# A state-space layer's constants: the elementwise work put on VectorE alone, and the lag products laid side by side on TensorE's columns

## The chip, the cores and the metric

The kernel runs on one core of one Trainium2 chip. The metric is the device time of one execution in microseconds. The kernel before takes 2569.31 us, the median of three runs (2568.99 to 2569.63). Five engines work beside each other, each through its own list of instructions in order: TensorE (PE; its weight loads are PEld), VectorE (DVE), ScalarE (ACT), GpSimd (POOL) and SyncE (SP), which issues most of the transfers. They wait for each other by semaphores.

## The reference, cut to what matters

A trunk of four residual layers on 512 positions of 1024 channels. Each layer has a token mixer (Fourier, state space, attention, Fourier) and a SwiGLU feed-forward. The change concerns the state-space mixer (S5) of the second layer, and of it only what depends on the parameters alone: the discretised diagonal system of 64 groups of 16 channels with 64 complex states, in two directions.

```python
def _s5_direction(u, lam_re, lam_im, log_dt, b_re, b_im, c_re, c_im, reverse):
    lam = lax.complex(lam_re, lam_im)
    dt = jnp.exp(log_dt)[:, None]
    lam_bar = jnp.exp(lam * dt)
    b_bar = ((lam_bar - 1.0) / lam)[..., None] * lax.complex(b_re, b_im)
    bu = lax.complex(einsum('bsgp,gnp->bsgn', u, b_bar.real), einsum('bsgp,gnp->bsgn', u, b_bar.imag))
    _, hs = lax.associative_scan(combine, (broadcast(lam_bar), bu), axis=1, reverse=reverse)
    return einsum('gpn,bsgn->bsgp', c, hs).real

y = y_fwd + y_bwd + d_skip * h        # then GELU and a gated linear unit
```

The kernel takes the 512 positions in 64 chunks of 8. Inside a chunk an output depends on an input at a distance (lag) of 0 to 7 positions, before it or behind it, through a 16 x 16 matrix per group and lag: C lam_bar^lag B, for each direction. These matrices, the input weights, the output weights and the angles of the states are what the preparation computes and stores in DRAM.

## The kernel before, in words

All activations lie with channels on the 128 partitions and the 512 positions along the free axis. The layers run one after the other. A feed-forward (`ffn`) has two halves; each half has 11 pairs of products for gate and up (`gemm`, 24 matmuls of 128x128 against 512 columns: 8 steps of three, since each weight is split into a high and a low float32r part), and then 8 blocks of the down product (33 matmuls each). The `Stream` loads a weight chunk of 512 KB into one of three buffers; ScalarE casts it to the high part (`whi`, line 191), VectorE subtracts to get the low part (`wlo`, line 192). When product n is issued, chunk n + 2 is split, and its buffers are those that product n - 1 read.

The preparation of the state-space layer (`s5_prepare`) is a list of closures. Six run in the Fourier layer before; the others are background work of the first feed-forward: `run_bg` is called after each product of the first half and the second, and pops closures at the rate of their number over 54 calls. With 57 closures, three calls pop two. The first 14 compute factors and powers of lam_bar; then come steps over 16 batches b of four groups, as a pipeline: step i issues stages of batches i, i - 1, i - 2 and so on, in two closures.

- `loads(b)`: three transfers on SyncE's queue (`xpw`, `xbj` of 512 KB, `bc` of 128 KB).
- `pool_part(b)`: six products and differences on GpSimd (angles `mph`, halves of the input weights `wtmp`, halves of the readers `ct`), with one rounding on VectorE between them.
- `dve_part(b)`: the input weights `wout`, four operations of 128x512 on VectorE.
- `dve_part2(b)`: the factor times B (`bt`), then `s5bd` by directions, four operations of 64x64; then the readers `ce`, four operations of 128x576.
- `lags(b)`: 8 products of 32 x 144 on TensorE, which the hardware runs as 16 instructions (lines 963 to 966), two copies by ScalarE into `lt` with both directions on 32 partitions, and the stores of `wout`, `mph`, `ce`.
- `lag0(b)`, `last(b)`: one direction's lag 0 is moved by a transfer to the other's partitions, VectorE adds it and the skip term (three operations of 16x64), and the rows go to DRAM (`s5ZS`), from where they are read skewed.

VectorE's order in a pair of the feed-forward is: `wlo`, the product of gate and up (line 500), one closure, `wlo`, two products from PSUM with the norm's factor (lines 474, 477), one closure. All the elementwise helper operations have line 733, so they are told apart by their tiles.

Of the kernel before, what the change touches and what calls it, by code (L numbers as in the profile page):

```python
# [16 lines left out]
P = 128  # L17
# [17 lines left out]
# ---------------------------------------------------------------- host layout  # L35
# [10 lines left out]
def _constants():  # L46
# [3 lines left out]
    c["ones"] = np.ones((P, P), f)  # L50
    bo = np.zeros((P, P), f)
# [13 lines left out]
    # positions 2u and 2u + 1 against the frequencies to 128, and the position 256  # L65
# [39 lines left out]
def _host_arrays(v):  # L105
# [44 lines left out]
    a["d5"] = cc(v["s5_d"][0].reshape(G5, 16).T)  # L150
# [65 lines left out]
class Net:  # L216
# [45 lines left out]
    # ---- weights in order of use  # L262
# [51 lines left out]
    def run_bg(self, slots):  # L314
        """Background work, spread over the slots that are left."""
# [8 lines left out]
    def keep_warm(self, count):  # L324
        """Matmuls without a use, so that TensorE's clock isn't halved by the wait that follows."""
# [10 lines left out]
    def gemm(self, hi, lo, chunk=None, ps=None, ks=range(KT)):  # L336
        """The next chunk's 128 columns against all of hi + lo."""
# [7 lines left out]
    # ---- residual stream and norms  # L345
# [4 lines left out]
    def mirrored(self, m):  # L350
        """Places of H for the positions: those above 256 backwards, 512 - s at 256 + s."""
# [3 lines left out]
    def start(self, nxt):  # L355
        """The first layer's input, as it comes in."""
# [19 lines left out]
    def after_x(self, m, nxt, late=None, defer=False):  # L376
# [38 lines left out]
        else:  # L415
# [5 lines left out]
            if late:  # L421
                # high part on ScalarE; VectorE takes the next sum before it waits for that
# [10 lines left out]
    def next_h(self):  # L433
        """A second place for the next layer's input."""
# [17 lines left out]
    # ---- feed forward  # L452
# [44 lines left out]
    def split_mul(self, hi, lo, t1, t2):  # L497
        """hi + lo = t1 * t2."""
# [5 lines left out]
    # ---- Fourier mixing  # L504
    def fnet(self, l, nxt):
        nc, H, j = self.nc, self.H, l // 3
        with ExitStack() as st:
# [12 lines left out]
            # the positions s = 2u and 2u + 1, then 512 - s for the odd and for the even ones. Position  # L520
            # 256, in the place of 512, is not to be folded: its row is taken apart.
# [6 lines left out]
            # block by block as the input comes in, for the first three tiles of tokens; the last  # L528
            # tile's products then run beside the norm's factors
# [24 lines left out]
            # the factors of the mirrored positions, in their order; zero at the place of 512  # L554
# [10 lines left out]
            def middle(hf, last):  # L565
                """Position 256."""
# [17 lines left out]
            def spread(u, ps, c):  # L584
                """The frequencies above 128 from those below."""
# [30 lines left out]
            def product(m, c):  # L616
                """The mixed channels' product with 128 columns of the weights."""
# [80 lines left out]
    # ---- S5: constants from the parameters, kept in DRAM until layer 1  # L698
# [21 lines left out]
    def s5_prepare(self):  # L720
        """Closures that each issue a part of the preparation."""
# [13 lines left out]
        def begin():  # L735
# [5 lines left out]
            for n in ("er", "ei", "er-"):  # L741
                T(n, [P, 9, 64], keep=True)
            for i in range(2):
                G.memset(T(f"bd{i}", [P, 2, 4, 2, 16], keep=True), 0.0)
            sm["iota"] = self.const("iota", pools["keep"])
            sm["lam"] = self.const("lam", pools["tmp"])
            sm["d5"] = self.const("d5", pools["keep"])
# [26 lines left out]
        def pexp1(x, scale=1.0):  # L774
            """exp(scale * x), to float32's accuracy, begun: x = k ln 2 + r."""
# [44 lines left out]
        def factors1():  # L820
            """(exp(lambda dt) - 1) / lambda."""
# [20 lines left out]
        def factors3():  # L842
            """One chunk's turn back, for the shift of the states."""
# [7 lines left out]
        def powers(ks):  # L851
            def go():
# [61 lines left out]
        def pool_part(b):  # L914
            d = tmp[b]
            pr, pi, xr, xi = d["we"]
            t = d["wt"] = tl("wtmp", [P, 2, 4, P])
            ph = d["ph"] = tl("mph", [P, 4, 64], 3)
            phi = sm["phi0"][:, 4 * b:4 * b + 4]
            tt(G, ph, phi.unsqueeze(2).to_broadcast([P, 4, 64]), sm["iota"].unsqueeze(1).to_broadcast([P, 4, 64]), M)  # L920
            x = t[:, 0, :, 0:64]
# [8 lines left out]
        def dve_part(b):  # L930
            d = tmp[b]
            pr, pi, xr, xi = d["we"]
            w = d["w"] = tl("wout", [P, 4, 2, P], 2)
            tt(V, w[:, :, 0], pr, xr, M)
            tt(V, w[:, :, 0], w[:, :, 0], d["wt"][:, 0], Sb)
            tt(V, w[:, :, 1], pr, xi, M)
            tt(V, w[:, :, 1], w[:, :, 1], d["wt"][:, 1], A)

        def dve_part2(b):
            d = tmp[b]  # L940
            bc = d["bc"]
# [9 lines left out]
            tt(V, ce[:, :, 0], e(b, "er"), c(d, 0), M)  # L951
            tt(V, ce[:, :, 0], ce[:, :, 0], d["ct"][:, 0], Sb)
            tt(V, ce[:, :, 1], e(b, "er-"), c(d, 1), M)
            tt(V, ce[:, :, 1], ce[:, :, 1], d["ct"][:, 1], Sb)

        def lags(b):
            k, h = divmod(b, 2)
            d = tmp[b]
            ce, bd = d["ce"], sm[f"bd{b % 2}"]
            lt = d["lt"] = tl("lt", [32, 4, 9, 16], 2)  # L960
            for g0 in (0, 2):
                ps = self.pst.tile([32, 2, 144], F32, name="pt", tag="pt")
                for g in range(g0, g0 + 2):
                    for ri in range(2):
                        nc.tensor.matmul(ps[:, g - g0, :], bd[:, ri, g].rearrange("p d q -> p (d q)"),
# [787 lines left out]
```

## Time and profile before

| what | value |
|---|---|
| median of three runs | 2569.31 us |
| span of the profiled execution | 2565.2 us (4.1 us less than that median) |
| mean granted TensorE clock | 0.976 |
| busy share PE, DVE, ACT, POOL | 95%, 54%, 34%, 25% |
| first feed-forward, 60 to 519 us | 459 us |
| last feed-forward, 2201 to 2561 us, no background work | 360 us |

In the tables of stretches each engine has its busy time in us and, in brackets, its number of instructions; PEclk is the granted clock as a share of full speed. In a timeline a row is a start, a duration, the engine, the line, the operation, what it writes and reads, shapes, and a count; in square brackets stands the engine's idle time before it and what ended it. Durations of neighbours overlap a little, so the cost of an operation is read from start to start.

### The profile page before, as it was taken

The numbers are of one execution on the slowest core, as the hardware profiler recorded it, in microseconds if no ns is written. First come the engines' busy times: TensorE is split into PE (matmuls) and PEld (weight loads), VectorE is DVE, ScalarE is ACT, GpSimd is POOL, SyncE is SP. The second block draws the span as 40 slices with busy tenths as digits, with TensorE's granted clock in tenths as the row PEclk, the third lists the DMA queues.
The fourth block names the chain that finished last, engine by engine and source line by source line (L and its number), as shares of the span: only waits on it lengthen the run. The fifth ranks groups of instructions, "written<-read, shape, count | busy, mean of one in ns | idle before, by whom it ended". The sixth has DMA issues, their size and how long they took to land.

```text
span 2565.2 us, 31445 instructions
## 1 busy us (share of the span) xinstructions
PE 2446.1 (95%) x12330; PEld 2034.3 (79%) x12330; DVE 1394.7 (54%) x2143; ACT 871.8 (34%) x1515; POOL 629.6 (25%) x496
## 2 busy tenths in 40 slices
PE   9999978968998999999999999989999999999999
PEld 7777756857887787889888797877888888788887
DVE  7669999487542334462754646556433444543332
ACT  3322112434232223342644526354322322332231
POOL 4464554142110001121332323322110112310010
PEclk9999988989999999999999999999999999999999
DMA  4246876683226463322132322313322222222222
GB/s 148 91 138 208 243 208 193 209 287 118 97 102 100 122 128 118 108 75 66 58 91 66 91 66 66 91 50 91 107 99 99 98 93 97 85 96 99 99 98 83
DMA packets 137944, 293.80 MB, mean 115 GB/s; under 512 B 32449, under 2 KB 73508, under 8 KB 137796
## 3 DMA queue, kind: packets, MB, share of 16 engines
q1 hardware_dynamic: 136316, 288.09, 36.8%
q10 hardware_dynamic: 1480, 3.70, 0.5%
q8 instruction: 97, 1.59, 0.3%
q14 instruction: 51, 0.42, 0.1%
HBM read 259.66 MB, written 36.21 MB: 115 GB/s over the span
## 4 chain that ended last, share of the span: by engine, by line
PE 72%; DVE 15%; ACT 5%; DMA 3%; issue 3%; POOL 3%; SPq 0%; ACTq 0%; DVEq 0%; POOLq 0%
PE pg L332 19%; PE pg L334 19%; PE pg L333 19%; DVE wlo L192 3%; PE pg L1377 2%; PE pg L1376 2%; PE pg L1375 2%; DMA w<-in_wdn_dram 1%; ACT whi L191 1%; DMA w<-in_wgu_dram 1%; DVE s5bd L733 1%; ACT p L1469 1%; DVE wout L733 1%; DVE ce L733 1%; DVE ms L1115 1%
## 5 line engine op out<-in xcount | busy, mean ns | idle before, releaser
L192 DVE TENSOR_TENSOR wlo<-w,whi 128x1024 fp32r<-128x1024 f32 x360 | 484.1, 1348 | 613.3 <-ACT whi L191 606.4
L334 PE MATMUL pg<-HH,wlo 128*128 128x512 f32 x1792 | 709.7, 396 | 40.7 <-DVE wlo L192 40.7
L332 PE MATMUL pg<-HH,whi 128*128 128x512 f32 x1792 | 715.0, 399 | 7.9 <-ACT whi L191 4.5
L333 PE MATMUL pg<-HH,whi 128*128 128x512 f32 x1792 | 707.4, 395 | 2.1 <-DVE HH L419 2.1
L191 ACT CAST whi<-w 128x1024 fp32r<-128x1024 f32 x360 | 376.2, 1048 | 583.0 <-PE pg L333 408.6
L334 PEld LDWEIGHTS pg<-HH,wlo 128*128 128x128 f32 x1792 | 342.1, 191 | 118.7 <-DVE wlo L192 46.2
L332 PEld LDWEIGHTS pg<-HH,whi 128*128 128x128 f32 x1792 | 342.8, 191 | 88.0 <-ACT whi L191 5.7
L333 PEld LDWEIGHTS pg<-HH,whi 128*128 128x128 f32 x1792 | 342.4, 191 | 75.2 <-DVE HH L419 4.5
L502 POOL TENSOR_TENSOR act<-t,act 128x512 fp32r<-128x512 f32 x88 | 116.2, 1321 | 937.0 <-ACT act L501 889.3
L332 PE MATMUL pg<-act,whi 128*128 128x512 f32 x704 | 276.1, 392 | 11.0 <-ACT whi L191 10.5
L333 PE MATMUL pg<-act,whi 128*128 128x512 f32 x704 | 275.5, 391 | 1.6 <-POOL act L502 1.6
L334 PE MATMUL pg<-act,wlo 128*128 128x512 f32 x704 | 275.3, 391 | 0.0
L332 PEld LDWEIGHTS pg<-act,whi 128*128 128x128 f32 x704 | 132.9, 189 | 40.7 <-ACT whi L191 10.9
L333 PEld LDWEIGHTS pg<-act,whi 128*128 128x128 f32 x704 | 133.0, 189 | 30.4 <-POOL act L502 3.0
L334 PEld LDWEIGHTS pg<-act,wlo 128*128 128x128 f32 x704 | 132.8, 189 | 28.3 <-DVE wlo L192 0.8
L477 DVE TENSOR_TENSOR t<-pg,r 128x512 f32<-128x512 f32 x88 | 60.5, 688 | 166.9 <-PE pg L334 166.9
L1408 POOL TENSOR_TENSOR qsl<-qsq,qsh 128x512 fp32r<-128x512 f32 x48 | 63.1, 1315 | 310.3 <-DVE qsh L1406 271.7
L475 ACT ACTIVATE t<-t 128x512 f32<-128x512 f32 x88 | 55.6, 632 | 245.7 <-DVE t L474 240.2
L1375 PE MATMUL pg<-whi,HH 128*128 128x256 f32 x384 | 138.3, 360 | 0.0
L1377 PE MATMUL pg<-wlo,HH 128*128 128x256 f32 x384 | 137.5, 358 | 0.0
L1376 PE MATMUL pg<-whi,HH 128*128 128x256 f32 x384 | 137.5, 358 | 0.0
L501 ACT CAST act<-t 128x512 fp32r<-128x512 f32 x88 | 54.6, 621 | 221.9 <-DVE t L500 221.9
(331 smaller groups left out, 3181.4 us busy)
## 6 DMA issues: line engine op xcount, KB each, us to landing
w<-in_wgu_dram SPq DMA_DIRECT2D x176, 512.0 KB, 3.3
w<-in_wdn_dram SPq DMA_DIRECT2D x88, 512.0 KB, 3.3
w<-in_wqk_dram SPq DMA_DIRECT2D x48, 512.0 KB, 3.3
w<-in_wv_dram SPq DMA_DIRECT2D x24, 512.0 KB, 3.2
xpw<-s5SC SPq DMA_DIRECT2D x16, 512.0 KB, 7.4
xbj<-in_bj_dram SPq DMA_DIRECT2D x16, 512.0 KB
s5WE<-wout SPq DMA_DIRECT2D x16, 512.0 KB, 5.0
s5YW<-ce SPq DMA_DIRECT2D x16, 512.0 KB, 6.7
```

The lines of the kernel that those rows point to most:

```text
L191: nc.scalar.copy(hi, t)
L192: nc.vector.tensor_tensor(lo, t, hi, ALU.subtract)
L332: mm(ps, wh, hh, start=first, stop=False)
L333: mm(ps, wh, hl, start=False, stop=False)
L334: mm(ps, wl, hh, start=False, stop=last)
L477: nc.vector.tensor_tensor(t2, pp[1], self.r, ALU.mult)
L502: nc.gpsimd.tensor_tensor(lo, t1, hi, ALU.subtract)
L733: e.tensor_tensor(o, x, y, op)
L1375: mm(ps, x, wh[:, k], start=(kk == 0 and t % 2 == 0), stop=False, skip_group_check=True)
L1376: mm(ps, y, wh[:, k], start=False, stop=False, skip_group_check=True)
L1377: mm(ps, x, wl[:, k], start=False, stop=(kk == 7), skip_group_check=True)
L1408: G.tensor_tensor(sl, sq, sh, SB)
```

## The change

`pool_part`, `dve_part` and `dve_part2` become `inputs(b)` (angles and input weights) and `readers(b)` (`bd` and `ce`), all on VectorE. The powers of lam_bar (48 operations of 128x128) go from GpSimd to VectorE, and six copies from GpSimd to ScalarE. The tile `bd` gets three forms, both directions and each one alone, on 32 columns of which 16 are zeros; two ScalarE copies fill the single ones. `lags` multiplies four groups on four blocks of 32 columns of TensorE, in three ranges of lags, so that both directions' lag 0 are added in PSUM and each group's rows come out on its own partitions in final order. ScalarE copies all but lag 0, VectorE adds the skip term to lag 0 from PSUM. `lag0` is gone, `last` only stores, four transfers in place of two. The pipeline has 19 steps in place of 21, the list 53 closures in place of 57: one for each call of `run_bg`.

```diff
             for i in range(2):
-                G.memset(T(f"bd{i}", [P, 2, 4, 2, 16], keep=True), 0.0)
+                G.memset(T(f"bd{i}", [P, 3, 2, 4, 32], keep=True), 0.0)
...
-                        tt(G, x, pr[:, k - 1], sm[u], M)
-                        tt(G, y, pi[:, k - 1], sm[v], M)
-                        tt(G, o[:, k], x, y, op)
+                        tt(V, x, pr[:, k - 1], sm[u], M)
+                        tt(V, y, pi[:, k - 1], sm[v], M)
+                        tt(V, o[:, k], x, y, op)
...
-                G.tensor_copy(o[0:64], s[0:64])
...
+                nc.scalar.copy(o[0:64], s[0:64])
...
+            tt(V, sm["dd"], sm["eyes"].unsqueeze(1).to_broadcast([P, 16, 16]),
+               sm["d5"].unsqueeze(2).to_broadcast([P, 16, 16]), M)
...
-        def pool_part(b):
+        def inputs(b):
...
-            tt(G, ph, ph, x, Sb)
-            tt(G, t[:, 0], pi, xi, M)
-            tt(G, t[:, 1], pi, xr, M)
-            t = d["ct"] = tl("ct", [P, 2, 4, 9, 16])
-            tt(G, t[:, 0], e(b, "ei"), c(d, 1), M)
-            tt(G, t[:, 1], e(b, "ei"), c(d, 0), M)
...
+            tt(V, ph, ph, x, Sb)
+            w = d["w"] = tl("wout", [P, 4, 2, P], 2)
+            for ri, (u, v, op) in enumerate(((xr, xi, Sb), (xi, xr, A))):
+                tt(V, w[:, :, ri], pr, u, M)
+                tt(V, t, pi, v, M)
+                tt(V, w[:, :, ri], w[:, :, ri], t, op)
...
+            tt(V, bd[:, 0, 0, :, 0:16], t[:, 0, 0], t[:, 1, 1], Sb)
+            tt(V, bd[:, 0, 1, :, 0:16], t[:, 1, 0], t[:, 0, 1], A)
             for di in range(2):
                 hs = slice(64 * di, 64 * di + 64)
-                tt(V, sm[f"bd{b % 2}"][hs, 0, :, di, :], t[hs, 0, 0], t[hs, 1, 1], Sb)
-                tt(V, sm[f"bd{b % 2}"][hs, 1, :, di, :], t[hs, 1, 0], t[hs, 0, 1], A)
+                nc.scalar.copy(bd[hs, 1 + di, :, :, 0:16], bd[hs, 0, :, :, 0:16])
...
+            for ri, n in enumerate(("er", "er-")):
+                tt(V, ce[:, :, ri], e(b, n), c(d, ri), M)
+                tt(V, t, e(b, "ei"), c(d, 1 - ri), M)
+                tt(V, ce[:, :, ri], ce[:, :, ri], t, Sb)
...
+            ps = self.pst.tile([P, 256], F32, name="pt", tag="pt")
+            for i, o, es in ((2, 0, slice(2, 9)), (0, 112, slice(0, 1)), (1, 128, slice(1, 8))):
+                for ri in range(2):
+                    for g in range(4):
+                        x = ce[:, g, ri, es].rearrange("p e q -> p (e q)")
+                        nc.tensor.matmul(ps[32 * g:32 * g + 32, o:o + 16 * (es.stop - es.start)], bd[:, i, ri, g], x,
+                                         start=(ri == 0), stop=(ri == 1))
+            cut = [t.rearrange("p (a x) -> p a x", a=2)[:, :, 0:112] for t in (lt, ps)]
+            nc.scalar.copy(*cut)
+            tt(V, lt[:, 112:128], ps[:, 112:128], sm["dd"][:, b], A)
...
+            lt = tmp.pop(b)["lt"]
+            for g in range(4):
+                nc.sync.dma_start(self.ZS[k, :, 4 * h + g], lt[32 * g:32 * g + 16, 0:240])
...
-        for i in range(21):
-            out.append(step(i, ((5, last), (4, lag0), (2, dve_part2))))
-            out.append(step(i, ((3, lags), (2, dve_part), (1, pool_part), (0, loads))))
+        for i in range(19):
+            out.append(step(i, ((3, last), (1, readers))))
+            out.append(step(i, ((2, lags), (1, inputs), (0, loads))))
```

On VectorE, the closure with the readers, between two low parts in the second half of the first feed-forward, reads so in the kernel before (`l` is what `lag0` brought back, `dd` the skip term):

```order
L500 TENSOR_TENSOR t_2746<-t_2746,t_2749 128x512
L733 TENSOR_TENSOR lt<-lt,l_2701 16x4x16
L733 TENSOR_TENSOR dd<-c_ident,c_d_333 16x64
L733 TENSOR_TENSOR lt<-lt,dd 16x4x16
L733 TENSOR_TENSOR bt<-bc,s5fr_318 128x2x64
L733 TENSOR_TENSOR bt<-bc,s5fi_320 128x2x64
L733 TENSOR_TENSOR s5bd_327<-bt 64x4x16 x4
L733 TENSOR_TENSOR ce<-s5er,bc 128x4x144
L733 TENSOR_TENSOR ce<-ce,ct 128x4x144
L733 TENSOR_TENSOR ce<-s5er-_324,bc 128x4x144
L733 TENSOR_TENSOR ce<-ce,ct 128x4x144
L192 TENSOR_TENSOR wlo<-w_2627,whi 128x1024
```

and so in the changed kernel, at the same place:

```order
L481 TENSOR_TENSOR t_2684<-pg,r 128x512
L737 TENSOR_TENSOR bt<-bc,s5fr_318 128x2x64
L737 TENSOR_TENSOR bt<-bc,s5fi_320 128x2x64
L737 TENSOR_TENSOR s5bd_327<-bt 128x4x16 x2
L737 TENSOR_TENSOR ce<-s5er,bc 128x4x144
L737 TENSOR_TENSOR ct<-s5ei,bc 128x576
L737 TENSOR_TENSOR ce<-ce,ct 128x4x144
L737 TENSOR_TENSOR ce<-s5er-_324,bc 128x4x144
L737 TENSOR_TENSOR ct<-s5ei,bc 128x576
L737 TENSOR_TENSOR ce<-ce,ct 128x4x144
L196 TENSOR_TENSOR wlo<-w_2519,whi 128x1024
```

Three operations on 16 partitions and two of the four `s5bd` are gone; the two `ct` products have come from GpSimd.

The other closure of the pair, with the input weights, on VectorE, before:

```order
L477 TENSOR_TENSOR t_2876<-pg,r 128x512
L733 TENSOR_TENSOR wout<-xpw,xbj 128x4x128
L733 TENSOR_TENSOR wout<-wout,wtmp 128x4x128
L733 TENSOR_TENSOR wout<-xpw,xbj 128x4x128
L733 TENSOR_TENSOR wout<-wout,wtmp 128x4x128
L922 TENSOR_SCALAR wtmp<-mph 128x4x64
L192 TENSOR_TENSOR wlo<-w_2719,whi 128x1024
```

and now, where `lt` is the skip term's addition from PSUM:

```order
L504 TENSOR_TENSOR t_2684<-t_2684,t_2687 128x512
L737 TENSOR_TENSOR lt<-pt,s5dd 128x16
L737 TENSOR_TENSOR mph<-s5phi_316,c_iota 128x256
L932 TENSOR_SCALAR wtmp<-mph 128x4x64
L737 TENSOR_TENSOR mph<-mph,wtmp 128x256
L737 TENSOR_TENSOR wout<-xpw,xbj 128x4x128
L737 TENSOR_TENSOR wtmp<-xpw,xbj 128x512
L737 TENSOR_TENSOR wout<-wout,wtmp 128x4x128
L737 TENSOR_TENSOR wout<-xpw,xbj 128x4x128
L737 TENSOR_TENSOR wtmp<-xpw,xbj 128x512
L737 TENSOR_TENSOR wout<-wout,wtmp 128x4x128
L196 TENSOR_TENSOR wlo<-w_2574,whi 128x1024
```

Two products and a difference for the angles and the two `wtmp` products have come from GpSimd, and the addition from PSUM stands ahead of them.

On TensorE the lag products of one batch stand between two feed-forward products; before (8 rows that are two instructions each in the trace):

```order
L333 MATMUL pg<-HH,whi 128x512
L334 MATMUL pg<-HH,wlo 128x512
L965 MATMUL pt<-ce,s5bd_327 32x144 x8
L332 MATMUL pg<-HH,whi 128x512
L333 MATMUL pg<-HH,whi 128x512
```

and now, at the same place:

```order
L337 MATMUL pg<-HH,whi 128x512
L338 MATMUL pg<-HH,wlo 128x512
L972 MATMUL pt<-ce,s5bd_327 32x112 x8
L972 MATMUL pt<-ce,s5bd_327 32x16 x8
L972 MATMUL pt<-ce,s5bd_327 32x112 x8
L336 MATMUL pg<-HH,whi 128x512
L337 MATMUL pg<-HH,whi 128x512
```

Eight products of 144 columns have become 24 of 112 and 16 columns, on four blocks of the array in turn.

## Rows read from the trace of the kernel before

**Rows 1.** Busy time by stretch, first feed-forward, then the last one.

```profile
core 0: us, PE busy (x) PEld busy (x) DVE busy (x) ACT busy (x) POOL busy (x), PEclk, DMA share, GB/s
82.00:203.40 121.40, 115.91 (x500) 94.31 (x499) 82.19 (x121) 34.35 (x44) 63.14 (x80) 0.97 0.42 127
203.40:274.00 70.60, 69.51 (x329) 55.70 (x328) 65.66 (x91) 16.50 (x23) 34.60 (x27) 1.00 0.76 228
274.00:459.30 185.30, 158.54 (x705) 124.19 (x704) 172.03 (x236) 40.57 (x65) 88.53 (x68) 0.92 0.73 214
...
2201.20:2322.10 120.90, 120.90 (x532) 99.75 (x532) 49.41 (x58) 40.54 (x48) 14.18 (x12) 1.00 0.29 96
2322.10:2381.90 59.80, 59.80 (x265) 49.51 (x265) 19.64 (x20) 12.27 (x13) 1.29 (x1) 1.00 0.28 97
```

**Rows 2.** Timeline of VectorE, one pair (start, us, line, operation).

```profile
305.51 0.68 DVE L474 TENSOR_TENSOR t<-pg,r 128x512 f32<-128x512 f32 x1
...
306.71 0.91 DVE L733 TENSOR_TENSOR lt<-lt,l 16x64 f32<-16x64 f32 x1
...
309.98 0.27 DVE L733 TENSOR_TENSOR bt<-bc,s5fr 128x128 f32<-128x128 f32 x1
...
310.48 1.64 DVE L733 TENSOR_TENSOR s5bd<-bt 64x64 f32<-64x64 f32 x4
312.16 0.76 DVE L733 TENSOR_TENSOR ce<-s5er,bc 128x576 f32<-128x576 f32 x1
...
315.23 1.22 DVE L192 TENSOR_TENSOR wlo<-w,whi 128x1024 fp32r<-128x1024 f32 x1
316.36 0.69 DVE L500 TENSOR_TENSOR t<-t,t 128x512 f32<-128x512 f32 x1
316.97 0.68 DVE L733 TENSOR_TENSOR wout<-xpw,xbj 128x512 f32<-128x512 f32 x1
...
318.29 1.78 DVE L733 TENSOR_TENSOR wout<-xpw,xbj 128x512 f32<-128x512 f32 x1
...
322.55 0.68 DVE L474 TENSOR_TENSOR t<-pg,r 128x512 f32<-128x512 f32 x1
```

**Rows 3.** Timeline of GpSimd in the same pair.

```profile
306.26 2.52 POOL L733 TENSOR_TENSOR wtmp<-xpw,xbj 128x512 f32<-128x512 f32 x2
308.74 2.80 POOL L733 TENSOR_TENSOR ct<-s5ei,bc 128x576 f32<-128x576 f32 x2
317.78 1.74 POOL L502 TENSOR_TENSOR act<-t,act 128x512 fp32r<-128x512 f32 x1 [6.24 <-ACT act L501]
```

**Rows 4.** Timeline of VectorE, two places where GpSimd stands still.

```profile
176.23 0.73 DVE L733 TENSOR_TENSOR s5bd<-bt 64x64 f32<-64x64 f32 x4
...
460.91 0.21 DVE L733 TENSOR_TENSOR lt<-lt,l 16x64 f32<-16x64 f32 x1
```

**Rows 5.** Timeline of TensorE: waits for a low part, one batch's lag products.

```profile
196.57 0.50 PE L334 MATMUL pg<-HH,wlo 128*128 128x512 f32 x1 [3.57 <-DVE wlo L192]
...
305.89 2.15 PE L965 MATMUL pt<-ce,s5bd 128*32 128x144 f32 x16
...
316.50 0.50 PE L334 MATMUL pg<-HH,wlo 128*128 128x512 f32 x1 [2.34 <-DVE wlo L192]
...
349.35 0.79 PE L334 MATMUL pg<-HH,wlo 128*128 128x512 f32 x1 [8.91 <-DVE wlo L192]
```

**Rows 6.** Timeline of TensorE in the state-space mixer, products on two column blocks.

```profile
555.66 2.29 PE L1088 MATMUL pg<-U,w 128*64 128x64 f32 x64 [1.38 <-DVE mtmp L1097]
557.78 0.39 PE L1154 MATMUL pt<-tg,U 128*64 128x128 f32 x4
...
558.43 0.39 PE L1154 MATMUL pt<-tg,U 128*64 128x128 f32 x4
```

**Rows 7.** Timeline of SyncE's queue, one issue of the store of `ce`.

```profile
317.83 1.78 SPq L970 DMA_DIRECT2D s5YW<-ce  x1
```

**Rows 8.** Transfers from 274 to 459 us: KB each, median us to landing.

```profile
s5YW<-ce SPq DMA_DIRECT2D x11, 512.0 KB, 6.1
```

More of the change, by code (lines that the diff above doesn't have):

```diff
@@ L50, in _constants @@
     c["ones"] = np.ones((P, P), f)
+    c["eyes"] = np.tile(np.eye(16, dtype=f), (8, 1))
     bo = np.zeros((P, P), f)
@@ L149, in _host_arrays @@
     a["bc"] = cc(np.stack(bn + cn, 2)).reshape(P, 8, 512)
-    a["d5"] = cc(v["s5_d"][0].reshape(G5, 16).T)
+    t = np.zeros((4, 2, 16, 16), np.float32)
+    t[:, 0] = v["s5_d"][0].reshape(16, 4, 16).transpose(1, 2, 0)
+    a["d5"] = t.reshape(P, 16)
     return a
@@ L743, in begin @@
             for i in range(2):
-                G.memset(T(f"bd{i}", [P, 2, 4, 2, 16], keep=True), 0.0)
+                G.memset(T(f"bd{i}", [P, 3, 2, 4, 32], keep=True), 0.0)
             sm["iota"] = self.const("iota", pools["keep"])
             sm["lam"] = self.const("lam", pools["tmp"])
-            sm["d5"] = self.const("d5", pools["keep"])
+            for n in ("d5", "eyes"):
+                sm[n] = self.const(n, pools["keep"])
+            T("dd", [P, 16, 16], keep=True)
             for n in ("dt", "t", "t2", "k", "rr", "yy", "e8", "x", "y"):
@@ L882, in exps @@
                 o, s = sm[n], sm[s][:, :, 0]
-                G.tensor_copy(o[0:64], s[0:64])
-                G.tensor_copy(o[64:128, 0], s[64:128, 0])
-                G.tensor_copy(o[64:128, 1:9], s[64:128, 8:0:-1])
+                nc.scalar.copy(o[0:64], s[0:64])
+                nc.scalar.copy(o[64:128, 0], s[64:128, 0])
+                nc.scalar.copy(o[64:128, 1:9], s[64:128, 8:0:-1])
+            tt(V, sm["dd"], sm["eyes"].unsqueeze(1).to_broadcast([P, 16, 16]),
+               sm["d5"].unsqueeze(2).to_broadcast([P, 16, 16]), M)
             V.tensor_scalar(sm["er-"], sm["er"], -1.0, None, M)
@@ L912, in c, with readers @@
             return d["bc"][:, 2 + i].unsqueeze(2).to_broadcast([P, 4, 9, 16])
-        def pool_part(b):
+        def inputs(b):
             d = tmp[b]
             pr, pi, xr, xi = d["we"]
-            t = d["wt"] = tl("wtmp", [P, 2, 4, P])
-            ph = d["ph"] = tl("mph", [P, 4, 64], 3)
+            t = tl("wtmp", [P, 4, P])
+            ph = d["ph"] = tl("mph", [P, 4, 64], 2)
             phi = sm["phi0"][:, 4 * b:4 * b + 4]
-            tt(G, ph, phi.unsqueeze(2).to_broadcast([P, 4, 64]), sm["iota"].unsqueeze(1).to_broadcast([P, 4, 64]), M)
-            x = t[:, 0, :, 0:64]
+            x = t[:, :, 0:64]
+            tt(V, ph, phi.unsqueeze(2).to_broadcast([P, 4, 64]), sm["iota"].unsqueeze(1).to_broadcast([P, 4, 64]), M)
             V.tensor_scalar(x, ph, MAGIC, -MAGIC, A, A)
-            tt(G, ph, ph, x, Sb)
-            tt(G, t[:, 0], pi, xi, M)
-            tt(G, t[:, 1], pi, xr, M)
-            t = d["ct"] = tl("ct", [P, 2, 4, 9, 16])
-            tt(G, t[:, 0], e(b, "ei"), c(d, 1), M)
-            tt(G, t[:, 1], e(b, "ei"), c(d, 0), M)
-        def dve_part(b):
-            d = tmp[b]
[L932 to L941, printed above, removed]
+            tt(V, ph, ph, x, Sb)
[4 more added lines that the diff above has]
+                tt(V, w[:, :, ri], w[:, :, ri], t, op)
+        def readers(b):
+            d = tmp[b]
+            bc, bd = d["bc"], sm[f"bd{b % 2}"]
             fr, fi = (sm[n][:, 4 * b:4 * b + 4].unsqueeze(2).to_broadcast([P, 4, 16]) for n in ("fr0", "fi0"))
@@ L945, in dve_part2 @@
             tt(V, t[:, :, 1], bc[:, 0:2], fi.unsqueeze(1).to_broadcast([P, 2, 4, 16]), M)
+            tt(V, bd[:, 0, 0, :, 0:16], t[:, 0, 0], t[:, 1, 1], Sb)
+            tt(V, bd[:, 0, 1, :, 0:16], t[:, 1, 0], t[:, 0, 1], A)
             for di in range(2):
                 hs = slice(64 * di, 64 * di + 64)
-                tt(V, sm[f"bd{b % 2}"][hs, 0, :, di, :], t[hs, 0, 0], t[hs, 1, 1], Sb)
-                tt(V, sm[f"bd{b % 2}"][hs, 1, :, di, :], t[hs, 1, 0], t[hs, 0, 1], A)
+                nc.scalar.copy(bd[hs, 1 + di, :, :, 0:16], bd[hs, 0, :, :, 0:16])
+            t = tl("ct", [P, 4, 9, 16])
             ce = d["ce"] = tl("ce", [P, 4, 2, 9, 16], 2)
[L951 to L954, printed above, removed]
+            for ri, n in enumerate(("er", "er-")):
+                tt(V, ce[:, :, ri], e(b, n), c(d, ri), M)
+                tt(V, t, e(b, "ei"), c(d, 1 - ri), M)
+                tt(V, ce[:, :, ri], ce[:, :, ri], t, Sb)
         def lags(b):
@@ L959, in lags @@
             ce, bd = d["ce"], sm[f"bd{b % 2}"]
[L960 to L965, printed above, removed]
-                                         ce[:, g, ri].rearrange("p e q -> p (e q)"), start=(ri == 0), stop=(ri == 1))
-                nc.scalar.copy(lt[:, g0:g0 + 2].rearrange("p g e q -> p g (e q)"), ps)
+            lt = d["lt"] = tl("lt", [P, 256], 2)
+            ps = self.pst.tile([P, 256], F32, name="pt", tag="pt")
[8 more added lines that the diff above has]
+            tt(V, lt[:, 112:128], ps[:, 112:128], sm["dd"][:, b], A)
             nc.sync.dma_start(self.WE[k, h], d["w"].rearrange("p g r n -> p (g r n)"))
```

14 lines of the change are left out of this document (removed).

## The prediction

> **What bounds the kernel now.** I read the stretches first. The first feed-forward holds the preparation, the last one nothing but itself, with the same products [rows 1]. The second half's gate-and-up products take 185.3 us with it and 120.9 without; the first half's down products 70.6 against 59.8. From 82 us on, 20 of the first half's 22 products remain: 121.4 against 20/22 of 120.9, 109.9. In these three stretches the preparation costs 64.4 + 10.8 + 11.5 = 87 us. In the long one VectorE is busy for 172 of 185 us, while TensorE is not: there VectorE sets the pace.
>
> The timeline of TensorE shows how: it stands 2.3 us before the matmul that takes a new low part, 8.9 us where a call has issued two closures, 3.6 us in another such place [rows 5]. One pair of products takes VectorE from 305.51 to 322.55, 17.05 us [rows 2], while TensorE needs 120.9/11 = 11.0 for it and 2.1 for a batch's lag products [rows 5]. The mean clock of 0.92 there [rows 1] is a result of these stops: TensorE falls back to its lower level after them, and gets no slower end from it, as it then waits for VectorE anyway.
>
> Last I laid GpSimd's timeline beside VectorE's. `wout` at 318.29 takes 1.78 us, its equal at 316.97 0.68; the longer one ends when GpSimd's `act` (317.78 to 319.52) does [rows 2, 3]. Four `s5bd` take 1.64 us beside the `ct` products and 0.73 where GpSimd is idle; `lt` takes 0.91 and 0.21 [rows 2 to 4]. The operations on line 474, which read PSUM, stay at 0.68. So in `dve_part2` and `last` VectorE pays for GpSimd's instructions with its own time.
>
> The Trainium skill says the same: a VectorE instruction with two SBUF inputs and a GpSimd instruction that reads SBUF exclude each other for a whole instruction ("SBUF — State Buffer", Who interferes with whom). "Perfetto Trace Analysis", Optimizing Scalar/DVE Operations, has a rule against the change: a saturated VectorE may be relieved by offloading, even to GpSimd. By that, taking 6 operations of a batch back costs time here, the third rival; the same paragraph doubts it for these two engines, as do the rows above.
>
> **VectorE's work, now and then.** Read from start to start. The feed-forward's own part of a pair: two low parts of 1.13 (315.23 to 316.36) and three products of 0.61 (316.36 to 316.97), 4.1 us [rows 2].
>
> - Readers: `bt` twice 0.5 (309.98 to 310.48); two of the four `s5bd`, undisturbed, 0.37 [rows 4], twice as wide in partitions, which does not count; six operations of 128x576 instead of four, of 3.07/4 = 0.77 (312.16 to 315.23), 4.6. Sum 5.5.
> - Inputs: six of 128x512 instead of four, 0.66 each (316.97 to 318.29 is two), 4.0. Three on the angles of 128x256; no row on VectorE: above 0.25 each (`bt`, 128x128) and under 0.66. I take 0.37, nearer the lower in size: 1.1. Sum 5.1.
> - Skip term: one of 128x16 from PSUM, 0.2 as the small one in [rows 4]. `dd`, both `lt` additions (3.3 us from 306.71 to 309.98) and half of `s5bd` are gone.
> - GpSimd keeps `act`, one in a pair: 1.78 - 0.68 = 1.1. Bounds: nothing, and its 1.7 whole.
>
> Pair: 4.1 + 5.5 + 5.1 + 0.2 + 1.1 = 16.0 us against 17.05. VectorE takes over work worth 3.8 us and still gets shorter. It remains the bound.
>
> **TensorE's lag products.** 16 instructions of 144 columns in 2.1 us are 0.13 each [rows 5]. Now 32 of 112 and 16 of 16 columns: at 0.10 and 0.02 one after the other 3.5 us. On two column blocks the mixer's 12 instructions of 128 columns take 0.65 us (557.78 to 558.43), 54 ns each, half of 0.13 x 128/144; 64 of 64 columns take 2.1, 33 ns [rows 6]. So blocks do run beside each other. Four blocks are not shown. If they run together: 8 rounds of 0.10 and 4 of 0.02 and 0.3 for filling, 1.2 us; with only two at once 2.0. I take 1.2, the bounds are 0.9 and 3.5. The Trainium skill gives about 60 cycles as a matmul's least ("TensorEngine Tiling (Array Packing)", Instruction Overhead), by which the sixteen short ones cost an estimated 0.4 us one after another and a quarter of that in fours; the sum would not differ by more than 0.1 in a batch.
>
> **The sum.** By the order, the second half has 9 readers and 10 inputs and no call with two closures.
>
> - Second half's products: after the last down product, VectorE has an addition 0.6, readers 5.5, a low part 1.1: 7.2. Then 9 pairs of 16.0, 144. Then a product, skip term, inputs, `act` and a low part, 8.1; then TensorE's last product, 5.0 after the low part is there. 164.3 instead of 185.3: 21.0 less. Here the lag products lie under VectorE's time.
> - First half's down products: VectorE has for two blocks 3.1 low parts, 1.2 additions and 10.8 (no `act` there): 15.1; TensorE 59.8/4 + 1.2 = 16.1. TensorE bounds. 59.8 + 4 x 1.2 + 1 for the start = 65.6, 5.0 less.
> - First half's products from 82 us: 109.9, one batch's lags 1.2, and 2 for stops. The readers and inputs of two batches push VectorE behind by some 4 us a pair, twice, and two products ahead cover most of that. 113.1, 8.3 less. The 48 small operations of the powers come to VectorE in four closures, 12 x 0.25 = 3 us each, beside a pair in which it has 11.0 - 4.1 us free: nothing. If not covered, up to 12.
>
> ScalarE's six copies and two more per batch lie in its idle time (40.6 us busy of 185 [rows 1]); its new wait for `s5bd` has the next high part queued behind it, which VectorE needs only after 4.6 us of readers. VectorE's new wait for the lag products in PSUM has the inputs and the next low part behind it; VectorE is late there, so the products are done. Both cost 0; if VectorE ever is early, the low part comes 7.5 us after the lags, and two products (11) cover it. Four small stores instead of two and one load less: SyncE's time, about even. The mixer itself reads the same tables: 0.
>
> 34.3 us less. The profiled execution's span is 2565.2, so it would be 2530.9; the runs' median is 4.1 above that span, so 2569.3 - 34.3 = **2535 us**.
>
> **Rivals.**
>
> 1. *The blocks do not run beside each other.* 3.5 instead of 1.2 in every batch: 4 + 1 batches where TensorE bounds, 12 us, and 2 at the end. 2549. Against it the mixer's rows.
> 2. *The stretched times stay* because GpSimd was not their reason. A pair is then 17.05 - 3.3 - 0.8 + 3.8 = 16.7: 3 us less in nine pairs, 9 for the double call, 5 and 3 in the other stretches: 2549. Against it the pairs of equal operations in rows 2 and 4.
> 3. *Offloading was right:* VectorE's stretched operations only filled waits that it has anyway, and GpSimd's work, 3.8 us a batch, comes on top in the 13 batches where VectorE bounds or nearly does: +49, less 12 for the double calls and 4 for lag products. About 2602, slower. With 172 of 185 us busy VectorE has hardly a wait to fill, so it is weak.
> 4. *VectorE stops for the store of `ce`,* slower too. The readers write the buffer whose store was issued in the closure just before. The store is issued 1.4 us after the low part (316.36 to 317.83) and lands 6.1 later, 7.5 [rows 2, 7, 8]; the next write of `ce`, one pair after 312.16, is at 329.2, 12.8 after the low part; in the changed order it comes after product, skip, inputs, `act`, low part, two products and `bd`, 10.2. A reserve of 2.7 instead of 5.3, while transfers, busy for 0.73 of the stretch [rows 1], get busy for 0.73 x 185.3/164.3 = 0.82. Twice the landing time costs 3.4 in 13 batches, 44: 2579. From 2.6 us of extra wait in a batch on, the whole gain is gone.
>
> **The numbers.** The forecast 0.74, rival 1 0.08, rival 2 0.06, rivals 3 and 4 0.07 together, no net change 0.03, better than all bounds 0.02. The forecast's own range: `act` at nothing gives 10 less, the angles at their upper bound 8 more, no stops 4 less; 2518 to 2547. With rivals 1 and 2, 2516 to 2552 holds 8 in 10. What counts as no change is within 0.2%, 5 us: faster 0.90, same 0.03, slower 0.07.
>
> **What would show it.** In the profile after: `s5bd`, `bt` and `ce` at their undisturbed times; GpSimd with `act` alone in the stretch; a pair of the second half at 15 to 16.5 us with VectorE without gaps; stops of TensorE of 2 to 4 us there, none of 9; 48 lag instructions in 1 to 1.5 us; the three stretches at 113, 66 and 164 us. Wrong: TensorE without stops in the second half (then VectorE was cheaper than I say), gaps on VectorE that a transfer or TensorE ends, lag products over 2 us.

## The result and the profile after

The changed kernel takes 2588.91 us (median of four runs, 2583.9 to 2591.64) against 2569.15 us of the kernel before in the same session: ratio 1.0075, 95% interval 1.0059 to 1.0091. It is 20 us slower, where 34 us less were forecast. The profiled execution took 2591.64 us, its span is 2589.8 us.

The stretches of the first feed-forward after, with the columns of [rows 1] (their ends have moved with the work):

```profile
82.00:197.90 115.90, 113.43 (x533) 92.30 (x532) 92.27 (x185) 37.22 (x52) 12.50 (x11) 0.99 0.38 119
197.90:271.90 74.00, 66.36 (x458) 52.29 (x457) 56.07 (x93) 17.21 (x27) 3.16 (x2) 1.00 0.68 204
271.90:477.40 205.50, 160.78 (x1058) 120.04 (x1056) 158.48 (x265) 42.68 (x72) 13.01 (x10) 0.86 0.67 197
```

The first stretch fell from 121.4 to 115.9, the way it was forecast but not as far (113.1). The down products rose from 70.6 to 74.0 (forecast 65.6), the second half's products from 185.3 to 205.5 (forecast 164.3). Together the three stretches are 18.1 us longer. VectorE's busy time in the long stretch has fallen from 172 to 158 us, but the stretch is 20 us longer: VectorE now stands still for 47 of its 205 us. So the loss is a wait.

VectorE's timeline after shows where, one pair (compare [rows 2]):

```profile
356.65 0.68 DVE L478 TENSOR_TENSOR t<-pg,r 128x512 f32<-128x512 f32 x1
...
360.47 0.29 DVE L737 TENSOR_TENSOR bt<-bc,s5fr 128x128 f32<-128x128 f32 x1 [2.54 <-DMA bc<-in_bc_dram]
...
361.00 0.36 DVE L737 TENSOR_TENSOR s5bd<-bt 128x64 f32<-128x64 f32 x2
361.28 0.75 DVE L737 TENSOR_TENSOR ce<-s5er,bc 128x576 f32<-128x576 f32 x1
...
365.54 1.22 DVE L196 TENSOR_TENSOR wlo<-w,whi 128x1024 fp32r<-128x1024 f32 x1
...
368.29 0.17 DVE L737 TENSOR_TENSOR lt<-pt,s5dd 128x16 f32<-128x16 f32 x1 [0.93 <-ACT lt L975]
368.38 1.33 DVE L737 TENSOR_TENSOR mph<-s5phi,c_iota 128x256 f32<-128x256 f32 x1
...
374.28 1.22 DVE L196 TENSOR_TENSOR wlo<-w,whi 128x1024 fp32r<-128x1024 f32 x1
375.41 0.68 DVE L478 TENSOR_TENSOR t<-pg,r 128x512 f32<-128x512 f32 x1
...
379.21 0.29 DVE L737 TENSOR_TENSOR bt<-bc,s5fr 128x128 f32<-128x128 f32 x1 [2.52 <-DMA bc<-in_bc_dram]
```

A pair is 18.76 us (356.65 to 375.41) where 17.05 stood before. The operations themselves are short: the readers take 5.07 us (360.47 to 365.54), with `s5bd`, `bt` and `ce` at their undisturbed durations. But the first reader stops 2.54 us for the load of `bc`, and the skip term 0.93 us for ScalarE.

SyncE's queue between the two readers (start, us, line, what is issued):

```profile
366.79 0.35 SPq L272 DMA_DIRECT2D w<-in_wgu_dram  x1
367.18 0.43 SPq L977 DMA_DIRECT2D s5WE<-wout  x1
367.66 0.43 SPq L978 DMA_DIRECT2D s5PH<-mph  x1
368.13 1.35 SPq L979 DMA_DIRECT2D s5YW<-ce  x1
369.53 0.98 SPq L909 DMA_DIRECT2D xpw<-s5SC  x1
370.55 1.32 SPq L910 DMA_DIRECT2D xbj<-in_bj_dram  x1
371.91 0.48 SPq L914 DMA_DIRECT2D bc<-in_bc_dram  x1
```

The weight load at 366.79 comes right after the low part of 365.54, as its buffer is free only then. Behind it in order stand three stores and two loads, and only then `bc`, 5.1 us later. It lands at 379.2, 7.3 us after its issue, and releases the next readers, and the next low part follows at their end. This is a closed loop: low part 1.25, queue 5.1, landing 7.3, readers 5.07: 18.7 us, which is the pair. The chain of waits runs along it (start, us, what), round after round:

```profile
365.54 1.23 DVE wlo L196
368.13 1.35 SPq L979
370.55 1.32 SPq L910
371.91 7.27 DMA bc<-in_bc_dram
381.48 1.43 DVE ce L737 x2
384.28 1.23 DVE wlo L196
```

In the kernel before, the first reader of `bc` was `ct` in `pool_part`, a whole step (two closures) behind `loads`. Now it is `readers`, in the very next closure. The sum of VectorE's stops from 82 to 540 us (engine, tile, what it waited for: us in sum, times, longest):

```profile
DVE bt L737 <- DMA bc<-in_bc_dram: 48.8, 13, 6.0
...
DVE lt L737 <- ACT lt L975: 9.7, 11, 0.9
```

TensorE's lag products take 1.10 us for 48 instructions, as forecast, in place of 2.15 [rows 5]; its stops behind the low part are 3.0 us at most, none is 9:

```profile
354.84 1.10 PE L972 MATMUL pt<-ce,s5bd 128*32 128x112 f32 x48
...
366.81 0.80 PE L338 MATMUL pg<-HH,wlo 128*128 128x512 f32 x1 [2.95 <-DVE wlo L196]
```

After such a stop TensorE runs at the lower of its two clock levels for a while (a matmul each 0.43 us from 367.40 on, each 0.23 before 361.70), and its granted clock in the long stretch is 0.86 in place of 0.92. That does not make the loss: from 271 to 461 us no instruction of TensorE stands in the chain of waits.

### The profile page after: what moved, and what is told of

The parts are those of the page before. It is cut to its first block, busy times and chain, and to the rows that moved or that the text cites. A ratio compares the mean times of both kernels' runs of the same rounds, so it can differ in the third digit from the quotient of the medians.

```text
span 2589.8 us, 32332 instructions
## 1 busy us (share of the span) xinstructions
PE 2450.3 (95%) x12842; PEld 2029.9 (78%) x12842; DVE 1381.0 (53%) x2224; ACT 878.1 (34%) x1537; POOL 471.6 (18%) x346
## 4 chain that ended last, share of the span: by engine, by line
PE 68%; DVE 14%; DMA 7%; ACT 5%; SPq 3%; issue 2%; POOL 0%; ACTq 0%; DVEq 0%; POOLq 0%
PE pg L336 18%; PE pg L338 18%; PE pg L337 18%; DMA bc<-in_bc_dram 4%; DVE wlo L196 3%; PE pg L1373 2%; PE pg L1372 2%; PE pg L1374 2%; DMA w<-in_wdn_dram 1%; DVE ce L737 1%; DMA w<-in_wgu_dram 1%; ACT whi L195 1%; ACT p L1466 1%; DVE ct L737 1%; PE pt L626 1%
```

## The experiments

The theory after the result: the loop through SyncE's queue and `bc` sets the pair. The rival: VectorE's work, or the transfers' bandwidth, is simply more than forecast. The runs come from several sessions; the kernel before took 2568.6 to 2569.9 us (medians) in each of them, so that their times can be set beside each other.

**`bc` issued first of the three loads.** In `loads` the lines of `bc` move ahead of those of `xpw` and `xbj`:

```diff
+            nc.sync.dma_start(bc.rearrange("p s g q -> p s (g q)"), src)
             nc.sync.dma_start(pw..., ...)
             nc.sync.dma_start(bj..., ...)
-            nc.sync.dma_start(bc.rearrange("p s g q -> p s (g q)"), src)
```

> The changed kernel with one thing moved: of the three loads of a batch, the small one of B and C (bc, 128 KB) is issued before the two of 512 KB instead of after them. Theory L (a loop sets the pair: low part done, SyncE's queue issues the stores and the loads, bc lands, VectorE's readers, next low part): the loop now is 5.7 us of issuing + 6.8 to landing + 5.1 + 1.1 = 18.7; without the two large issues ahead of it (2.3 us) and with a shorter queue before its packets bc lands about 4 us earlier, VectorE's wait for bc goes from 2.5 us a pair to 0 or 0.5, a pair takes 16.2 to 16.7, the whole 2545 to 2558 us. Theory W (VectorE's larger work or the transfers' bandwidth is the bound, and the wait for bc only shows it): the wait moves to xpw or xbj, the pair stays at 18.5 or more, the time at 2583 to 2592.

Measured 2548.86 us, ratio 0.9919 (0.9904 to 0.9934). Moving one issue by two places gives 40 us. Waits for `bc` fall from 48.8 to:

```profile
DVE bt L737 <- DMA bc<-in_bc_dram: 16.2, 7, 4.5
```

**`bc` loaded a step ahead**, with a third buffer; `loads(b)` keeps the other two:

```diff
-            out.append(step(i, ((2, lags), (1, inputs), (0, loads))))
+            out.append(step(i, ((2, lags), (1, inputs), (0, loads), (-1, load_bc))))
```

> The changed kernel with bc loaded one step earlier than the two large loads of the same batch, into three buffers. Theory L: the wait for bc is gone wholly; a pair is VectorE's own 15.3 us and the 0.9 in which VectorE waits for ScalarE's copy of lt, 16.2; the second half's products take 166 us instead of 205, the down products of the first half 66 instead of 74; in all 2536 to 2546 us, faster than the kernel before. If it is no better than the load moved within its step, landing was early enough there. Theory W: no change, 2583 to 2592.

Measured 2546.02 us, ratio 0.9907 (0.9893 to 0.9922). But for one stop of 1.1 us no reader waits for `bc`; a pair takes 16.13 us (330.60 to 346.73), against 16.0 forecast for the change:

```profile
330.60 0.68 DVE L478 TENSOR_TENSOR t<-pg,r 128x512 f32<-128x512 f32 x1
...
339.60 0.17 DVE L737 TENSOR_TENSOR lt<-pt,s5dd 128x16 f32<-128x16 f32 x1 [0.93 <-ACT lt L978]
...
345.60 1.22 DVE L196 TENSOR_TENSOR wlo<-w,whi 128x1024 fp32r<-128x1024 f32 x1
346.73 0.68 DVE L478 TENSOR_TENSOR t<-pg,r 128x512 f32<-128x512 f32 x1
```

The same bytes move and VectorE does the same work, so work and bandwidth were not what made the pair 18.7. In place of the stops for `bc` a smaller wait appears, which the changed kernel does not have, the one of the prediction's fourth rival:

```profile
DVE ce L737 <- DMA s5YW<-ce: 8.7, 4, 3.6
```

**The skip term behind the input weights as well.** `inputs` is issued ahead of `lags` in a step:

```diff
-((2, lags), (1, inputs), (0, loads), (-1, load_bc))
+((1, inputs), (2, lags), (0, loads), (-1, load_bc))
```

> As the run with bc loaded a step earlier, and in a closure the inputs are issued before the lag products, so that VectorE's addition of the skip term stands behind its inputs. If the 0.9 us at which VectorE waits for ScalarE's copy of lt in each pair lies on the path, it goes: 15.3 us a pair, some 9 us less than the run with bc ahead alone, 2527 to 2537 us. If the feed-forward's act on GpSimd only meets another operation of VectorE instead, or the wait was covered, the same within 2 us.

Measured 2538.04 us (2536.23 to 2547.15), ratio 0.9887 (0.9867 to 0.9908): 8 us less again by the medians, and 1 us more than expected. One of its four times, 2547.15, lies with those of the run before, so the times alone carry the 8 us weakly; the pair carries it, 15.30 us, 0.83 less than in the run before it. VectorE's timeline:

```profile
343.06 0.68 DVE L478 TENSOR_TENSOR t<-pg,r 128x512 f32<-128x512 f32 x1
...
351.05 0.42 DVE L737 TENSOR_TENSOR mph<-s5phi,c_iota 128x256 f32<-128x256 f32 x1
...
352.18 1.79 DVE L737 TENSOR_TENSOR wout<-xpw,xbj 128x512 f32<-128x512 f32 x1
...
357.14 0.17 DVE L737 TENSOR_TENSOR lt<-pt,s5dd 128x16 f32<-128x16 f32 x1
...
358.36 0.68 DVE L478 TENSOR_TENSOR t<-pg,r 128x512 f32<-128x512 f32 x1
```

The stop before `lt` is gone from the pairs. GpSimd's `act` now stretches a `wout` (1.79) where it stretched `mph` (1.33). The stretches are 111.3, 68.2 and 165.4 us; the forecast was 113.1, 65.6 and 164.3.

**The same move without the earlier `bc`**, to see whether the two losses add up or one covers the other:

```diff
-((2, lags), (1, inputs), (0, loads))
+((1, inputs), (2, lags), (0, loads))
```

> The changed kernel with one edit: in a step, `inputs` is issued ahead of `lags`, so that VectorE's skip addition `lt`, which stops it 0.93 us for ScalarE in each pair, stands behind the input weights. The load of `bc` stays as it is in the changed kernel, last of three. Theory of the loop (low part, SyncE's queue, landing of `bc`, readers, low part = the period of 18.7 us): the addition is not in the loop, VectorE only waits longer for `bc`; pair 18.5 to 18.9 us, time 2585 to 2592 us, as the changed kernel, although the stops for `lt` (9.7 us in sum) are gone. Rival (VectorE's own time sets the pace, `lt` and `bc` are independent losses that add up): the same edit gave 8 us when `bc` was ahead, so 2581 us and a pair of 17.9 us.

Measured 2589.1 us, ratio 1.0078 (1.0063 to 1.0093): nothing gained. From reader to reader it is 18.78 us:

```profile
343.27 0.29 DVE L737 TENSOR_TENSOR bt<-bc,s5fr 128x128 f32<-128x128 f32 x1 [3.93 <-DMA bc<-in_bc_dram]
...
362.05 0.29 DVE L737 TENSOR_TENSOR bt<-bc,s5fr 128x128 f32<-128x128 f32 x1 [3.40 <-DMA bc<-in_bc_dram]
```

Of the 9.7 us of stops for `lt` 0.9 are left, and the rest has come back as stops for `bc`, 48.8 before this edit and now:

```profile
DVE bt L737 <- DMA bc<-in_bc_dram: 58.4, 13, 6.2
```

An edit worth 8 us off the loop is worth nothing while the loop stands. This is what shows the loop, more than the gain of the first two runs.

**`bc` first and the skip term late**, the first edit and the last one together:

```diff
+            nc.sync.dma_start(bc.rearrange("p s g q -> p s (g q)"), src)
             nc.sync.dma_start(pw..., ...)
             nc.sync.dma_start(bj..., ...)
-            nc.sync.dma_start(bc.rearrange("p s g q -> p s (g q)"), src)
...
-((2, lags), (1, inputs), (0, loads))
+((1, inputs), (2, lags), (0, loads))
```

> The run that issues `bc` first of the three loads, with `inputs` ahead of `lags` in a step as well. Theory of the loop: with `bc` first the loop is only 2.3 us shorter than in the changed kernel (18.7 - 2.3 = 16.4 at its landing time there), and the pair with `bc` first is 16.1, so the loop itself is at its limit; taking the stop for `lt` away then helps little, pair 15.6 to 16.1, time 2543 to 2549 us, with more waiting for `bc` than the 16 us of that run. Rival (`bc` first has already taken the load off the path): the full 8 us of the same edit on the kernel that loads `bc` a step ahead, 2540 us or less, waits for `bc` unchanged.

Measured 2545.8 us (2543.78 to 2549.52), ratio 0.9911 (0.9896 to 0.9926): 3 us less than `bc` first alone (2544.68 to 2549.3), which is within the spread of the two, and not 8; waits for `bc` rise from 16.2 us in 7 stops to 21.5 in 10. With `bc` first the loop is only just short enough.

**Two products of a batch back on GpSimd** (the `wtmp` pair, on the kernel that loads `bc` a step ahead; the rounding gets a tile of its own, `mphx`):

```diff
+            tt(G, t[:, 0], pi, xi, M)
+            tt(G, t[:, 1], pi, xr, M)
...
-                tt(V, t, pi, v, M)
```

> As the run with bc loaded a step earlier, but the two products wtmp of a batch (128x512 each) go back to GpSimd, so VectorE has 1.3 us of own work less in a batch. Theory S (VectorE's operations on two SBUF tiles are stretched to the end of GpSimd's instruction): GpSimd's two products take 2.5 to 3 us beside the angles and the first wout; these are stretched by at least the 1.3 us that VectorE gave away; the time is 0 to 15 us longer than with bc ahead alone. Theory O (offloading relieves VectorE): 1.3 us less in 13 batches, 10 to 17 us shorter.

Measured 2558.0 us, ratio 0.9953 (0.9939 to 0.9967), 12 us slower than the same kernel with these products on VectorE. VectorE's timeline:

```profile
330.23 0.17 DVE L737 TENSOR_TENSOR lt<-pt,s5dd 128x16 f32<-128x16 f32 x1 [0.93 <-ACT lt L979]
330.32 1.29 DVE L737 TENSOR_TENSOR mph<-s5phi,c_iota 128x256 f32<-128x256 f32 x1
331.64 1.26 DVE L937 TENSOR_SCALAR mphx<-mph 128x256 f32<-128x256 f32 x1
332.94 1.40 DVE L737 TENSOR_TENSOR mph<-mph,mphx 128x256 f32<-128x256 f32 x1
...
337.05 1.22 DVE L196 TENSOR_TENSOR wlo<-w,whi 128x1024 fp32r<-128x1024 f32 x1
```

and GpSimd's:

```profile
330.03 1.30 POOL L506 TENSOR_TENSOR act<-t,act 128x512 fp32r<-128x512 f32 x1 [12.93 <-DMA s5ZX<-s5ZS]
331.28 2.78 POOL L737 TENSOR_TENSOR wtmp<-xpw,xbj 128x512 f32<-128x512 f32 x2
```

From `lt` to the next low part it is 6.8 us (330.23 to 337.05) against 6.0 with all on VectorE (339.60 to 345.60 there). VectorE has 1.3 us of work less in between and still takes 0.8 longer, so the two products cost it 2.1 on GpSimd: the rounding takes 1.26 in place of 0.29, the difference 1.40 in place of 0.42, for as long as GpSimd's two products run. By the Trainium skill ("SBUF — State Buffer", Who interferes with whom) a VectorE instruction with two SBUF inputs contends with a GpSimd instruction that reads SBUF, over ports that one of them holds for its whole instruction; the same section says that a `tensor_scalar` can enter a mode that takes both ports as well. These rows agree on both, the difference and the rounding. The second and third rivals fall: the stretching is GpSimd's doing, as `s5bd` at its undisturbed time in the changed kernel also shows, and giving work back to GpSimd costs time.

**The last GpSimd operation, `act`, on VectorE too** (on the kernel with `bc` ahead and `lt` late; issued after the closure that follows its product; `split_mul` did it on GpSimd):

```diff
-                    self.split_mul(*late.pop())
+                    hi, lo, t1, t2 = late.pop()
...
+                    lows.append((lo, t1, hi))
...
+                    nc.vector.tensor_tensor(*lows.pop(), ALU.subtract)
```

> The best kernel so far (`bc` a step ahead, `inputs` ahead of `lags`), with the subtraction `act` of the feed-forward, the last operation of GpSimd in the stretch, on VectorE as well, after the closure that follows the product it belongs to. Theory (GpSimd's `act` costs VectorE 1.1 us by stretching one `wout` from 0.68 to 1.79, more than the 0.61 us that it takes on VectorE itself): `wout` at 0.68 everywhere, pair 15.3 - 1.1 + 0.6 = 14.8, nine pairs -4.5 us, time 2533 to 2535 us. The store of `ce` begins to stop the readers there (10.2 us in six waits already), which may eat half of it. Rival (a saturated VectorE only gets worse from more work): pair 15.9, about +5 us, 2543.

Measured 2532.28 us (2531.47 to 2533.21), ratio 0.9857 (0.9842 to 0.9871). Every `wout` of the pair is 0.68 or 0.69, the pair 14.79 us (341.38 to 356.17; 14.8 expected). The wait of the prediction's fourth rival, for the store of `ce`, has grown, from 10.2 us in the kernel that this one starts from to:

```profile
DVE ce L746 <- DMA s5YW<-ce: 12.5, 7, 3.9
```

**The store of `ce` issued first of the three stores** in `lags`, otherwise the kernel just told:

```diff
+            nc.sync.dma_start(self.YW[k, h]...)
             nc.sync.dma_start(self.WE[k, h], ...)
             nc.sync.dma_start(self.PH[k, ...], ...)
-            nc.sync.dma_start(self.YW[k, h]...)
```

> The best kernel so far (`bc` a step ahead, `inputs` ahead of `lags`, `act` on VectorE), with the store of `ce` issued first of a batch's three stores. Theory (the readers of the next batch but one step stop for that store, 12.5 us in seven waits, as the fourth rival of the prediction said, and 0.94 us of issuing `wout` and `mph` stands ahead of it): each wait gets 0.9 us shorter, the sum 12.5 falls to some 6, time 2526 to 2529 us. Rival (the stores share the transfer engines anyway, so that the place in the queue does not matter): waits unchanged, 2532 us.

Measured **2523.95 us** (2522.34 to 2524.64), ratio 0.982 (0.9804 to 0.9836), the fastest of all: 46 us under the kernel before, 65 under the changed one. The waits have halved:

```profile
DVE ce L746 <- DMA s5YW<-ce: 6.2, 3, 4.0
```

The time fell by 8.3 us, 2 more than the waits of VectorE; the cause of that rest is open. Its long stretch, in the columns of [rows 1]; TensorE's clock stays at its upper level there, 1.00 where the changed kernel has 0.86, and the transfers are busy for 0.84 of it in place of 0.67, so they were not the bound of the changed kernel:

```profile
261.10:418.00 156.90, 138.72 (x1058) 106.10 (x1056) 150.81 (x268) 42.96 (x72) 0.00 (x0) 1.00 0.84 258
```

**The lag products group by group** (two loops exchanged, on the kernel with `bc` ahead), so that neighbours in the list are on the same column block half of the time:

```diff
-                for ri in range(2):
-                    for g in range(4):
+                for g in range(4):
+                    for ri in range(2):
```

> The kernel that loads `bc` one step ahead, with the lag products issued group by group (for each of the four column blocks both of its products, then the next block) instead of block after block for each product. Theory (blocks run beside each other when neighbours in the list are on different blocks): neighbours are now on the same block half of the time, so a batch of 48 instructions takes about 2 us instead of 1.1; time the same to +3 us (2546 to 2549), since VectorE sets the pace of the second half and only the 4 batches in the down products and the first one show it. Rival (the short instructions are cheap by themselves): 1.1 us again.

Measured 2545.29 us, ratio 0.9906 (0.9889 to 0.9922), about the time that was expected. The batch is not as expected: I had expected 2 us.

```profile
203.96 1.24 PE L975 MATMUL pt<-ce,s5bd 128*32 128x112 f32 x48
```

So a second run on that kernel, with the same 48 instructions once more on a single block:

```diff
+                        nc.tensor.matmul(ps[0:32, o:o + 16 * (es.stop - es.start)], bd[:, i, ri, g], x,
+                                         start=(ri == 0), stop=(ri == 1))
```

> The kernel with the lag products in turn (48 instructions on four column blocks, 1.24 us a batch), with the same 48 instructions a second time, all on the first block of 32 columns, into columns of PSUM that nothing reads. Theory (the blocks run beside each other, whatever the order in the list): on one block they run one after the other, 32 x 0.10 + 16 x 0.02 = 3.5 us a batch. Rival (instructions of 112 columns on 32 of the array's columns are cheap by themselves): 1.2 us again. If the order mattered, as I had expected before, the first set would be at 2 us; it was at 1.24.

TensorE's timeline, a batch on four blocks (L975) and then on one (L981); some of the first set's instructions overlap the second:

```profile
203.15 1.17 PE L975 MATMUL pt<-ce,s5bd 128*32 128x112 f32 x46
...
204.16 3.64 PE L981 MATMUL pt<-ce,s5bd 128*32 128x112 f32 x47
```

3.64 us on one block against 1.2 on four: the blocks do run side by side, in either order of the list. The one time of this run, 2555.54 us, holds the added products and says nothing of the change.

## Why the prediction was wrong

The steps that sized the work held. Term by term, forecast and measured:

- Readers 5.5, measured 5.07; input weights with angles and `act` 6.2, measured 5.9 (368.38 to 374.28). Angles undisturbed 1.13 (351.05 to 352.18 in the run with `lt` late), 1.1 taken. One of the three, the rounding, did have a row on VectorE before the change (321.20, 0.29 us), which the prediction missed.
- `act` 1.1, measured 1.79 - 0.68 = 1.1; taking it off GpSimd shortened the pair by 0.5, which is 1.1 less its 0.6 on VectorE. The reading behind it was off: the long `wout` does not end with `act` but 0.55 us later (320.07 against 319.52, [rows 2, 3]).
- Lag products 1.2, of which the 0.3 for filling had no row behind it, measured 1.10; on one block 3.64, where 3.5 was worked out. The first rival is out.
- First half's products 113.1, measured 115.9 with the waits for `bc` and 111.3 without.
- First half's down products 65.6, 68.2 without those waits: the term for stops, 1 us, was too small there; TensorE stands for 2.9 of the 68.2.

Two sums do not come out by their own terms, and nothing turns on either: the work that VectorE takes over is 3.6 us (two `ct` of 0.77, two `wtmp` of 0.66, two of the angles of 0.37), not 3.8, and the bounds named for the forecast's own range give 2521 to 2543, not 2518 to 2547.

The step that failed is the one on VectorE's new waits. It named one, the lag products in PSUM, and put it at 0: "VectorE is late there, so the products are done". They were done, but the addition stood behind ScalarE's copy into the same tile `lt`, which is issued in the same closure behind ScalarE's own `act` copy: up to 0.93 us in 11 batches, 9.7 in all, worth 8 us once the loop was gone. The other wait, which cost 43 us (2588.9 to 2546.0), was not named at all. The prediction followed `ce` from its store to its next write in the fourth rival, and wrote of SyncE "about even". It did not ask the same of `bc`: the distance from its load to its first reader had shrunk from two closures to one. Of the signs of being wrong that it listed, "gaps on VectorE that a transfer or TensorE ends" is the one that came. The numbers for this were in the trace of the kernel before. Its queue took 5.5 us from the weight load behind a low part to the issue of `bc`:

```profile
316.47 0.36 SPq L268 DMA_DIRECT2D w<-in_wgu_dram  x1
...
321.94 0.44 SPq L905 DMA_DIRECT2D bc<-in_bc_dram  x1
```

The landing time of `bc` from 274 to 459 us was 7.7 us, as the view of its transfers says (in the columns of [rows 8]):

```profile
bc<-in_bc_dram SPq DMA_DIRECT2D x8, 128.0 KB, 7.7
```

An estimate, worked as the fourth rival was, with these 5.5 us of queue and 7.7 to land: `bc` is there 13.2 us after the low part. In the forecast's own order the readers come after a product 0.6, skip 0.2, inputs 5.1, `act` 1.1, a low part 1.1 and two products 1.2: 9.3. VectorE is 3.9 us early in each batch; in the 13 batches of that rival this is 51 us, and 2535 becomes 2586, slower than the kernel before. 2589 was measured.

The fourth rival had the right mechanism, VectorE stopping in the readers for a transfer that SyncE issues late, with the wrong transfer. Its own wait is not in the changed kernel; it came up as soon as `bc` was out of the way, 8.7 us at a pair of 16.1, then 10.2 at 15.3 and 12.5 at 14.8. With both new waits taken away the kernel takes 2538 us, where 2535 was forecast for the change. That the two agree so well is in part luck: the pair is 15.3 us where 16.0 was forecast, and the stops for `ce`, which the forecast put at nothing, take back what that saves.

## What to carry to other kernels

When a stage is moved earlier or a pipeline is shortened, list every tile that the moved stage reads and count the closures between its load and its first read, before and after; the new distance is to be held against queue plus landing time, for each tile and not only for the largest store. A small load issued last on an in-order queue, behind a transfer that waits for compute, can close a loop, and the length of the loop is then the pace of the stage (18.7 us here). While such a loop stands, other savings on the engine come back as waiting, so an edit that gains nothing alone may gain its full price afterwards.

## What the runs showed of the hardware

- A load of 128 KB took 7.2 to 8.3 us from issue to landing in the second half of the changed kernel, issued behind two loads of 512 KB. The first such load of the preparation took 3.8 us in the run with `lt` late, where it was issued ahead of them (161.39). So its size does not set its landing time; how much of it is the queue and how much the other transfers, these runs do not separate.
- Four blocks of 32 columns gave 48 instructions in 1.10 us against 3.64 on one block, and exchanging the loops so that neighbours share a block cost only 0.14.
- A VectorE operation of 0.29 us lasted 1.26 beside a GpSimd product of 1.39, more than four times its own time; one of 0.42 lasted 1.40, one of 0.68 beside `act` 1.79. Each of them gained about 1 us, so that small operations pay most for their size. They end after GpSimd's instruction, not with it: a `wout` of 0.68 us 0.56 us after `act` (353.97 against 353.41, run with `lt` late). Operations that read PSUM on line 474 stayed at 0.68 beside GpSimd (305.51, kernel before).
